# Entering a feed-forward layer with two plain hidden tiles instead of four: normalisation read from the banks, sums added by transfers

## The chip, the cores and the metric

The kernel runs on one core of one Trainium2 chip. The metric is the time of one execution on the device in microseconds (us). Nothing else runs on the core, and the inputs lie in HBM.

## What is computed

Two layers over 512 tokens with 1024 features each, all in float32. Each layer is a half-step feed-forward network (FFN), a mixer of three kinds of heads, and a second half-step FFN:

```python
def swiglu(h, w_in, w_out):
    gate, up = jnp.split(h @ w_in, 2, axis=-1)
    return (jax.nn.silu(gate) * up) @ w_out

for l in range(DEPTH):                      # DEPTH = 2
    x = x + 0.5 * swiglu(rms_norm(x, ffn1_norm[l]), ffn1_w_in[l], ffn1_w_out[l])
    h = rms_norm(x, mix_norm[l]) @ w_mix_in[l]
    y = concat([short_conv(h), hgrn2(h), fox_attention(h)])
    x = x + y @ w_mix_out[l]
    x = x + 0.5 * swiglu(rms_norm(x, ffn2_norm[l]), ffn2_w_in[l], ffn2_w_out[l])
```

`w_in` is 1024x5632 (2816 gate columns and 2816 up columns), `w_out` is 2816x1024. `rms_norm` divides each token by the root of its mean square over the 1024 features and multiplies by a gain for each feature.

## The kernel before, in words

The residual stream lies in SBUF with features on partitions: `xT` is eight tiles j of 128 features x 512 tokens. Float32 accuracy is kept with three products of the reduced type float32r: every operand is parted into a high part (a cast on ACT) and a low part (a subtraction on DVE), and `mm3` (L316 to L339) issues high x high (L328), high x low (L336) and low x high (L337). Two helpers make these pairs: `parted` (L314 ACT, L315 DVE) for streamed weights, `prepare` in `halved` (L810 ACT, L812 DVE) for weights that are sums.

An FFN has 22 hidden tiles of 128. Two ways to compute them stand in the code:

- **Plain.** A pair of hidden tiles takes 8 feature tiles x 4 banks (two gate, two up) x 3 = 96 matmuls of 512 tokens (`stream_steps`). The operand is x times gain (`scaled`, L402 to L415: ACT L408, DVE L409), and the division by the root of the mean square comes afterwards, from the bank (`clear`, `values`). So a plain pair needs no norm before it starts.
- **Halved.** A pair is computed by a scheme of seven block products P1 to P7 over halves of the features and of the tokens, in the order P1, P2, P6, P5, P7, P3, P4 (`ORDER_IN`); each product is 8 x 3 = 24 matmuls of 256 tokens, 168 for the pair. It needs the normed x cut into four quarters X[a,b] (a: half of the features, b: half of the tokens), sums of these quarters, and sums of four quarters of the weights. `plan` orders the products and gives loads, accumulating DMAs and sums their due places; `LEAD = 3` says that weights are parted three products ahead.

The first tiles of each FFN are plain because the norm of x isn't ready yet: they are the "covered" tiles. The very first FFN covers six (`FIRST`, its own function `cover`); the other three (FFN 2 of layer 0, FFN 1 and FFN 2 of layer 1) cover four, by `enter` (L583 to L699). These three places are called entries here.

An entry, before:

1. The last four banks of the phase ahead (the mixer's output projection, or the FFN's) hold the new contribution to features 512 to 1023. DVE adds each to `xT` (L1230 or L502), then ACT squares it (L424), DVE adds the square into `sqacc` (L425), and `scaled` makes the gained pair.
2. TensorE runs the first plain pair from the gained x. After the sixth of its eight feature tiles the sum of squares is parted (L438) and two matmuls with a matrix of 1/1024 give the mean to every partition (L447). ACT takes Ln, Exp and a square (L277) and DVE finishes the reciprocal root `inv` (L431 to L433).
3. During the second plain pair DVE multiplies the four quarters (L619, 16 instructions), adds them (L642), and ACT and DVE part P1, P2, P5, P6 (`high` L632, `low` L635 and L637). The raw weights of the first halved pair (four tiles of 512 KB) are loaded by SP (L863) and one is added to another by an accumulating DMA from POOL (L786).
4. The halved products begin. P7, P3 and P4 are made beside them (`self.entry`, by product number), and so are the values of the covered tiles.

What fixes the order: TensorE's, ACT's and DVE's instructions are queued in program order, with hand-set order among those marked by `follow`; an instruction waits for semaphores at the head of its queue. All PSUM banks are allotted in two groups of four (`next4`). Of the halved products P1, P6, P7 and P4 go into one bank (called a), P2 into a second (c), P5 and P3 into a third (b); ACT reads bank a after P1 (L919), and DVE reads it after P7 (L934), each before the next product may write it. Parted weights lie in a ring of three tiles `hl`, streamed weights in a ring of two tiles `st`.

Of the kernel before, what the change touches and what calls it, by code (L numbers as in the profile page):

```python
# [9 lines left out]
F32 = mybir.dt.float32  # L10
# [30 lines left out]
FIRST = 6  # L41
# [21 lines left out]
def plan(covered):  # L63
# [27 lines left out]
    for u in dict.fromkeys((k, w) for k, w, _ in seq):  # L91
# [68 lines left out]
class Trunk:  # L160
# [255 lines left out]

    def squared(self, j, xj, pool):
# [25 lines left out]

    def end_norm(self, bank, pool, parts, keep=False):
        nc = self.nc
        for n, part in enumerate(parts):
            nc.tensor.matmul(bank, self.ones_mean, part, start=n == 0, stop=n == 1)  # L447
# [10 lines left out]
    def ffn(self, w_in, w_out, next_gain, covered, begin=None, out=None):  # L458
        nc = self.nc
        tc = self.tc  # L460
        with tc.tile_pool(name=self.n("ffn"), bufs=1) as fp:
# [26 lines left out]
            for dg in range(2):  # L488
                banks = self.next4()

                def parts(k, kk, dg=dg):
# [4 lines left out]
                    [(bk, slice(c, c + P), None) for bk, c in zip(banks, (0, 128, 256, 384))],  # L496
                    parts, self.last_hidden, nf,
                )
                for i in range(4):
# [6 lines left out]
                    if next_gain is not None:  # L506
                        self.norm_part(j, fp)
# [75 lines left out]
    def enter(self, fp, w_in, then):  # L583
        nc = self.nc
        H = T // 2
        A, V = (lambda i, e=e: self.follow(e, i) for e in "av")

        def stream(f, banks, given):
            def parts(k, kk):
                r = slice(k * P, (k + kk) * P)  # L590
                return [w_in[r, f * P : (f + 2) * P], w_in[r, FF + f * P : FF + (f + 2) * P]]

            return self.stream_steps(
                [(bk, slice(c, c + P), None) for bk, c in zip(banks, (0, 256, 128, 384))],
                parts, self.xact, KD, given=given,
            )

        ba = self.next4()
        first = stream(0, ba, lambda k: k == KD - 2)
        for _ in range(4):  # L600
            next(first)
        parts = self.parted_norm(fp, ("g1", "g1"), 2, True)
        nb = self.bank("pt" if self.ntog % 2 == 0 else "po")
        bb = self.next4()
        second = stream(2, bb, lambda k: True)
        self.ngain = self.const.tile([P, KD], F32, tag="ngain", name=self.n("ngain"))
        A(nc.scalar.activation(self.ngain, self.gain, AF.Copy, scale=-1.0))
        next(second)
        self.end_norm(nb, fp, parts, True)
        self.table(SILU)  # L610
        next(first, None)
        next(then)
        X, self.xc, lows = {}, {}, {}

        def quarter(a, b):
# [28 lines left out]
        def both(name):  # L644
            high(name)
            lows[name]()

        def row():
            next(second)
            next(second, None)  # L650

        cleared = {}

        def clear(f, i):
            banks = bb if f else ba
            cleared[f, i] = self.clear(fp, banks[2 * i], banks[2 * i + 1], True)

        def values(f, i):
            self.values(fp, f, i, *cleared.pop((f, i)), True)

        quarter(0, 0)
        high("P1")
        quarter(1, 0)
        lows["P1"]()
        next(second)
        next(second)
        high("P2")
        quarter(0, 1)
        lows["P2"]()
        quarter(1, 1)  # L670
        next(second)
        next(second)
        add((0, 0), (0, 1))
        high("P5")
        clear(0, 0)
        lows["P5"]()
        next(second)
        next(second)
# [1244 lines left out]
```

## Time and profile before

| what | value |
|---|---|
| median of 3 runs | 1805.61 us (1802.3 to 1805.83) |
| the profiled execution | 1801.38 us |
| its span, first to last instruction | 1799.6 us |
| TensorE busy | 1792.0 us (100%) |
| DVE, ACT, POOL busy | 1430.1 us (79%), 1001.0 us (56%), 176.6 us (10%) |
| HBM, mean over the span | 126 GB/s |

The profile names TensorE PE, VectorE DVE, ScalarE ACT, GpSimd POOL and SyncE SP. PEld is PE's loading of held operands, which overlaps PE. A row of a group shows the line of the kernel, the engine, the operation, the tiles written and read, shape, count, then busy time and the mean in ns of one, then idle time before it and who ended it. A row of a timeline shows start in us from the start of the span, duration, and the same names; "x4" means four instructions merged into a row. Matmuls overlap in a pipeline, so the rate is read from one start to the next, not from the duration. L numbers in the profile are those of the kernel before.

The three entries lie at about 570 to 650 us, 895 to 975 us and 1460 to 1540 us of the span.

### The profile page before, as it was taken

The page shows a single profiled execution, that of the slowest core. Times are in us where ns is not written, and L with a number is a line of the kernel's source. Part 1 is how long each engine was busy: PE and PEld are TensorE (multiplying, and loading weights), DVE is VectorE, ACT ScalarE, POOL GpSimd, SP SyncE. Part 2 cuts the span into 40 slices and gives each one's busy share as a digit, 9 for nine tenths or more (in the row PEclk, how much of TensorE's full clock was granted, in tenths as well). Part 3 has the DMA queues.
Part 4 walks back from the last instruction along what each step waited for, and adds up shares of the span by engine and source line. Part 5 has one row for each costly group of instructions (what it writes and reads, how often), then busy time and mean ns, then how long its engine had stood idle before and what let it go on. Part 6 is the DMA issues. An engine that isn't in the chain of part 4 may idle for free.

```text
span 1799.6 us, 34747 instructions
## 1 busy us (share of the span) xinstructions
PE 1792.0 (100%) x14271; PEld 1681.0 (93%) x14271; DVE 1430.1 (79%) x2006; ACT 1001.0 (56%) x1445; POOL 176.6 (10%) x184
## 2 busy tenths in 40 slices
PE   9999999999999999999999999999999999999999
PEld 7899999899888899999889999998998888999997
DVE  9889787676888798879679887876868879888793
ACT  5455554464776465556446555555547755555551
POOL 0011120100000002112001111201000000020210
PEclk9999999999999999999999999999999999999999
DMA  7659793233433857868265786913334346597762
GB/s 207 180 133 196 169 188 97 71 82 84 106 98 108 222 130 170 194 163 166 82 207 133 169 185 175 187 65 83 78 85 116 89 144 179 141 185 190 160 133 94
DMA packets 244638, 254.09 MB, mean 141 GB/s; under 512 B 18904, under 2 KB 228576, under 8 KB 244480
## 3 DMA queue, kind: packets, MB, share of 16 engines
q1 hardware_dynamic: 189424, 182.38, 33.7%
q0 software_dynamic: 54752, 69.23, 23.8%
q8 instruction: 112, 1.84, 0.4%
q14 instruction: 46, 0.38, 0.1%
q10 hardware_dynamic: 304, 0.27, 0.0%
HBM read 223.98 MB, written 2.10 MB: 126 GB/s over the span
## 4 chain that ended last, share of the span: by engine, by line
PE 94%; DVE 2%; ACT 2%; DMA 1%; issue 1%; SPq 0%; POOL 0%; ACTq 0%; DVEq 0%; POOLq 0%
PE mm L328 14%; PE mm L336 14%; PE mm L337 14%; PE sc L328 6%; PE sc L336 6%; PE sc L337 6%; PE pt L336 6%; PE pt L328 6%; PE pt L337 6%; PE po L328 4%; PE po L336 4%; PE po L337 4%; PE po L1654 1%; PE pt L1698 1%; PE pt L1352 1%
## 5 line engine op out<-in xcount | busy, mean ns | idle before, releaser
L810 ACT CAST hl<-w 128x1024 fp32r<-128x1024 f32 x322 | 336.8, 1050 | 305.9 <-PE mm L337 80.4
L812 DVE TENSOR_TENSOR hl<-w,hl 128x1024 fp32r<-128x1024 f32 x322 | 391.8, 1220 | 96.7 <-ACT hl L810 96.7
L315 DVE TENSOR_TENSOR hl<-st,hl 128x512 fp32r<-128x512 f32 (+3 forms) x196 | 162.5, 830 | 116.2 <-ACT hl L314 115.0
L314 ACT CAST hl<-st 128x512 fp32r<-128x512 f32 (+3 forms) x196 | 143.1, 732 | 174.3 <-PE po L337 66.8
L328 PE MATMUL mm<-xc,hl 128*128 128x256 f32 (+1 forms) x733 | 201.3, 276 | 0.0
L336 PE MATMUL mm<-xc,hl 128*128 128x256 f32 x728 | 201.2, 276 | 0.0
L337 PE MATMUL mm<-xc,hl 128*128 128x256 f32 x728 | 201.0, 276 | 0.0
L328 PE MATMUL sc<-xc,hl 128*128 128x256 f32 (+1 forms) x532 | 146.0, 276 | 0.0
L336 PE MATMUL sc<-xc,hl 128*128 128x256 f32 x528 | 146.0, 276 | 0.0
L337 PE MATMUL sc<-xc,hl 128*128 128x256 f32 x528 | 145.8, 276 | 0.0
L328 PEld LDWEIGHTS mm<-xc,hl 128*128 128x128 f32 x733 | 137.4, 188 | 0.2
L337 PEld LDWEIGHTS mm<-xc,hl 128*128 128x128 f32 x728 | 136.7, 188 | 0.0
L336 PEld LDWEIGHTS mm<-xc,hl 128*128 128x128 f32 x728 | 136.7, 188 | 0.0
L328 PE MATMUL pt<-xc,hl 128*128 128x256 f32 (+1 forms) x482 | 132.6, 276 | 0.0
L336 PE MATMUL pt<-xc,hl 128*128 128x256 f32 x480 | 132.6, 276 | 0.0
L337 PE MATMUL pt<-xc,hl 128*128 128x256 f32 x480 | 132.5, 276 | 0.0
L328 PE MATMUL mm<-x,hl 128*128 128x512 f32 x272 | 107.6, 396 | 0.0
L336 PE MATMUL mm<-x,hl 128*128 128x512 f32 x272 | 106.3, 391 | 0.0
L337 PE MATMUL mm<-x,hl 128*128 128x512 f32 x272 | 106.2, 390 | 0.0
L328 PEld LDWEIGHTS sc<-xc,hl 128*128 128x128 f32 x532 | 99.7, 188 | 0.2
L336 PEld LDWEIGHTS sc<-xc,hl 128*128 128x128 f32 x528 | 99.1, 188 | 0.0
L337 PEld LDWEIGHTS sc<-xc,hl 128*128 128x128 f32 x528 | 99.1, 188 | 0.0
(517 smaller groups left out, 5575.0 us busy)
## 6 DMA issues: line engine op xcount, KB each, us to landing
w<-in_ffn_w_in_dram SPq DMA_DIRECT2D x140, 512.0 KB, 5.1
w<-in_ffn_w_out_dram SPq DMA_DIRECT2D x64, 512.0 KB, 5.2
w<-in_ffn_w_out_dram POOLq DMA_DIRECT2D x56, 512.0 KB, 7.2
st<-in_w_mix_in_dram SPq DMA_DIRECT2D x88, 256.0 KB, 2.8
st<-in_ffn_w_in_dram SPq DMA_DIRECT2D x70, 256.0 KB, 3.1
w<-in_ffn_w_in_dram POOLq DMA_DIRECT2D x35, 512.0 KB, 8.9
w<-S POOLq DMA_DIRECT2D x35, 512.0 KB, 4.7
st<-in_ffn_w_out_dram SPq DMA_DIRECT2D x24, 512.0 KB, 5.3
```

Of the source, the lines that this page charges most:

```text
L314: a = nc.scalar.copy(hi, src[:, c : c + w])
L315: b = nc.vector.tensor_sub(lo, src[:, c : c + w], hi)
L328: i = nc.tensor.matmul(acc[:, c], ah, bh[:, c], start=first and c.start == 0, stop=False, skip_group_check=True,)
L336: nc.tensor.matmul(acc, a, b, start=False, stop=False, skip_group_check=True)
L337: i = nc.tensor.matmul(acc, c, d, start=False, stop=last, skip_group_check=True)
L810: A(nc.scalar.copy(hi, src))
L812: return lambda: V(nc.vector.tensor_sub(lo, src, hi))
L1352: nc.tensor.matmul(bank[hh][rows[par], at + x * n : at + (x + 1) * n], held[rows[hh], c * CH : (c + 1) * CH], moving(rows[hh], c), start=T ...
L1654: nc.tensor.matmul(self.ob[:, t0 + u * P : t0 + 2 * P], V[:, j, h % 4].rearrange("p a d -> p (a d)"), part[:, j, u:, :].rearrange("p i t - ...
L1698: nc.tensor.transpose(tb[:, j * P : (j + 1) * P], p[:, j * P : (j + 1) * P], self.ident)
```

## The change

The three entries cover one plain pair instead of two (`COVERED = 2`), so that one more pair of each of these FFNs is halved. To that end:

- **Old x in the last banks** (`seed`): before the last four banks of the phase ahead accumulate, ACT copies the old `xT` of that feature tile into the bank (three banks of four after the mixer, four after the FFN, there with a factor of 2), and the matmuls add to it. The sum then stands in the bank.
- **Squares from the banks** (`norm_late`): ACT squares the bank itself, DVE adds the squares, and the copy of the bank to `xT` (`arrive`) comes later on ACT. For the last bank after the mixer DVE still adds to `xT` first. The gained pairs of features 512 to 1023 (`scaled`) move from ahead of the mean to behind the reciprocal root.
- **The mean** is put after the second feature tile of the one plain pair.
- **Quarters**: for two of four, ACT multiplies by the gain (`grown`, four instructions of 128x256) and DVE by `inv` in one instruction of 128x1024 (`multiplied`); the other two are made as before (`made`).
- **Early weights**: the loads of the first halved pair's raw weights are issued right after the first part of the plain pair. The FFN's pool of tiles gets `reuse_waits="tile"`.
- **Sums by accumulating transfers**: the sum S3 of the weights, and the sum X[0,1] + X[1,1] (`carry`), are made by accumulating DMAs on POOL's queue instead of DVE.

The core of the diff:

```diff
-FIRST = 6
+FIRST, COVERED = 6, 2
@@ plan
                 when(-1, 6, "adds", u)
-                when(0, 2, "total", u, "S3")
+                if covered == FIRST:
+                    when(0, 2, "total", u, "S3")
@@ new
+    def seed(self, js, banks, scale):
+        for j, bk in zip(js, banks):
+            if scale == 1.0:
+                self.nc.scalar.copy(bk, self.xT[:, j, :])
+            else:
+                self.nc.scalar.activation(bk, self.xT[:, j, :], AF.Copy, scale=scale)
+
+    def norm_late(self, js, pool, banks, scale, update=None):
...
+        for j, bk in zip(js, banks):
+            own = update is not None and j == js[-1]
+            if own:
+                self.follow("v", update(j, bk))
...
+            src = self.xT[:, j, :] if own else bk
+            self.follow("a", nc.scalar.activation(sq, src, AF.Square, scale=scale))
+            self.follow("v", nc.vector.tensor_add(self.sqacc, self.sqacc, sq))
+            self.arrive[j] = lambda j=j, bk=bk, own=own: own or self.follow(
+                "a", nc.scalar.activation(self.xT[:, j, :], bk, AF.Copy, scale=scale)
+            )
@@ ffn
-        with tc.tile_pool(name=self.n("ffn"), bufs=1) as fp:
+        with tc.tile_pool(name=self.n("ffn"), bufs=1, reuse_waits="tile") as fp:
@@ enter
+        def grown(a, b):
+            X[a, b] = t = fp.tile([P, 4, H], F32, tag=f"r{2 + 2 * a + b}", name=self.n("xn"))
+            for k in range(4):
+                i = 4 * a + k
+                A(nc.scalar.activation(
+                    t[:, k, :], self.xT[:, i, b * H : (b + 1) * H], AF.Copy,
+                    scale=(self.gain if a == b else self.ngain)[:, i : i + 1],
+                ))
+
+        def multiplied(a, b):
+            V(nc.vector.tensor_mul(
+                X[a, b], X[a, b], self.inv[:, b * H : (b + 1) * H].unsqueeze(1).to_broadcast([P, 4, H])
+            ))
...
+        def carry(x, y):
+            self.follow("g", nc.gpsimd.dma_start(X[x], X[y], accum_op=ALU.add))
...
+        next(plain)
+        next(then)
+        self.arrive[7]()
+        self.arrive[6]()
+        norm = self.parted_norm(fp, ("g1", "g1"), 2, True)
+        self.mean(nb, norm)
+        next(plain)
+        next(plain)
+        self.arrive[4]()
+        self.arrive[5]()
+        self.factor(nb, fp, True)
+        grown(0, 0)
+        multiplied(0, 0)
+        for j in (4, 5):
+            self.scaled(j, self.xT[:, j, :], True)
+        next(plain)
+        next(plain)
+        for j in (6, 7):
+            self.scaled(j, self.xT[:, j, :], True)
+        next(plain)
         high("P1")
-        quarter(1, 0)
+        grown(1, 0)
+        low = prepared(0)
         lows["P1"]()
...
+        multiplied(1, 0)
+        low()
+        self.given["total"]()
+        self.given["add"](0, 2)
         high("P2")
...
+        made(0, 1)
         lows["P2"]()
...
         add((0, 0), (0, 1))
+        low()
         high("P5")
...
+        made(1, 1)
         lows["P5"]()
...
+        carry((0, 1), (1, 1))
         add((0, 0), (1, 1))
         high("P6")
-        self.given["total"]()
         lows["P6"]()
...
         next(then)
...
         self.entry = {
-            0: lambda: both("P7"),
-            1: lambda: (both("P3"), add((0, 0), (1, 0))),
-            3: lambda: high("P4"),
-            7: lambda: values(0, 1),
-            9: lambda: clear(2, 0),
-            10: lambda: values(2, 0),
-            13: lambda: values(2, 1),
+            0: lambda: (high("P7"), lows["P7"]()),
+            1: lambda: (high("P3"), lows["P3"]()),
+            2: lambda: (add((0, 0), (1, 0)), high("P4"), lows["P4"]()),
+            8: lambda: clear(0),
+            9: lambda: values(0),
+            11: lambda: clear(1),
+            12: lambda: values(1),
         }
-        self.between = {4: lambda: lows["P4"](), 13: lambda: clear(2, 1)}
+        self.between = {}
```

How it moves instructions is shown at two places of the first entry. First PE's queue around the mean, `ones_mean` being the matrix of 1/1024, `x2` the gained pairs of the feature tiles, `hl` the parted weights. Before:

```order
L328 MATMUL pt_974_6817<-x2_965_6791,hl_980_6881 128x512
L336 MATMUL pt_974_6817<-x2_965_6791,hl_980_6881 128x512
L337 MATMUL pt_974_6817<-x2_965_6791,hl_980_6881 128x512
L447 MATMUL po_985_6918<-sh_983_6914,ones_mean_72 128x512
L447 MATMUL po_985_6918<-sh_984_6915,ones_mean_72 128x512
L328 MATMUL sc_971_6814<-x2_967_6798,hl_982_6911 128x512
```

and of the kernel with the change:

```order
L329 MATMUL pt_970_6805<-x2_948_6708,hl_974_6812 128x512
L337 MATMUL pt_970_6805<-x2_948_6708,hl_974_6812 128x512
L338 MATMUL pt_970_6805<-x2_948_6708,hl_974_6812 128x512
L469 MATMUL po_971_6806<-sh_979_6849,ones_mean_72 128x512
L469 MATMUL po_971_6806<-sh_980_6850,ones_mean_72 128x512
L329 MATMUL sc_967_6802<-x2_950_6715,hl_982_6858 128x512
```

The mean stood behind 72 matmuls of the plain pair (six feature tiles) and now stands behind 24 (two).

Second DVE's queue ahead of the third halved product, P6. `xc` are parted sums of quarters (P1, P2, P5, P6 in this order), `xn` the quarters, `S` the sum of weights that P6 takes, `gi`, `ui`, `hq` the values of a covered tile, `w` raw weights. Before, from the last streamed weights to the low part of P6's weights:

```order
L315 TENSOR_TENSOR hl_1017_7101<-st_1016_7098,hl_1017_7101 128x1024
L642 TENSOR_TENSOR xn_1000_6976<-xn_1000_6976,xn_1009_7029 128x1024
L798 TENSOR_TENSOR S_1020_7132<-w_996_6967,w_997_6969 128x1024
L637 TENSOR_TENSOR xc_1019_7130<-xn_1000_6976,xc_1018_7129 128x1024
L812 TENSOR_TENSOR hl_1021_7135<-w_997_6969,hl_1021_7135 128x1024
L812 TENSOR_TENSOR hl_1022_7138<-w_999_6973,hl_1022_7138 128x1024
L572 TENSOR_TENSOR gi_1023_7141<-pt_973_6816,inv_995_6937 128x512
L573 TENSOR_TENSOR ui_1024_7142<-pt_974_6817,inv_995_6937 128x512
L642 TENSOR_TENSOR xn_1008_7023<-xn_1008_7023,xn_1009_7029 128x1024
L713 TENSOR_TENSOR hq_1026_7150<-gi_1014_7068,ui_1015_7069 128x256
L710 SCALAR_TENSOR_TENSOR hq_1027_7152<-gi_1014_7068,ui_1015_7069 128x256
L812 TENSOR_TENSOR hl_1028_7154<-S_1020_7132,hl_1028_7154 128x1024
```

and of the kernel with the change, from the product with `inv` that makes the second quarter to the low part of P6's weights:

```order
L648 TENSOR_TENSOR xn_997_6977<-xn_997_6977,inv_987_6897 128x1024
L862 TENSOR_TENSOR hl_998_6982<-w_976_6841,hl_998_6982 128x1024
L848 TENSOR_TENSOR S_999_6987<-w_975_6839,w_976_6841 128x1024
L656 SCALAR_TENSOR_TENSOR xn_1003_6996<-xT_76,ngain_972_6807,inv_987_6897 128x256 x4
L674 TENSOR_TENSOR xc_1001_6991<-xn_997_6977,xc_1000_6990 128x1024
L679 TENSOR_TENSOR xn_988_6902<-xn_988_6902,xn_1003_6996 128x1024
L862 TENSOR_TENSOR hl_1002_6994<-w_978_6845,hl_1002_6994 128x1024
L656 SCALAR_TENSOR_TENSOR xn_1006_7007<-xT_76,gain_630_5444,inv_987_6897 128x256 x4
L674 TENSOR_TENSOR xc_1005_7005<-xn_988_6902,xc_1004_7004 128x1024
L679 TENSOR_TENSOR xn_988_6902<-xn_988_6902,xn_1006_7007 128x1024
L674 TENSOR_TENSOR xc_1008_7016<-xn_988_6902,xc_1007_7015 128x1024
L862 TENSOR_TENSOR hl_1010_7022<-S_999_6987,hl_1010_7022 128x1024
```

The weights of the second plain pair (`st`) and the values of covered tiles (`gi`, `ui`, `hq`) are gone from this stretch. The low parts of the three halved weights and their sum S stand between the quarters now. Between the reciprocal root and the first of these rows stand seven more: a 128x1024 product with `inv` (the first quarter), four gained pairs of 128x512, one streamed weight of 128x1024 and P1's low part of 128x1024.

More of the change, by code (lines that the diff above doesn't have):

```diff
@@ L642, in add @@
             V(nc.vector.tensor_add(X[x], X[x], X[y]))
[L644 to L661, printed above, removed]
+        held = {}
@@ L1229, in add @@
             def add(j, bank):
[L1230 removed]
+                return nc.vector.tensor_add(self.xT[:, j, :], bank, self.xT[:, j, :])
             def most():
```

106 lines of the change are left out of this document (52 added, 54 removed).

## The prediction

> **What bounds the kernel now.** I read the page first, for the bound over the whole span, then PE's waits.
>
> ```profile
> PE 1792.0 (100%) x14271; PEld 1681.0 (93%) x14271; DVE 1430.1 (79%) x2006; ACT 1001.0 (56%) x1445; POOL 176.6 (10%) x184
> PEclk9999999999999999999999999999999999999999
> PE pt L1698 <- DVE QA L1600: 1.3, 2, 0.6
> PE mm L1815 <- DVE z L1802: 1.2, 1, 1.2
> ...
> PE po L447 <- ACT sh L438: 0.2, 1, 0.2
> ```
>
> PE is busy in the whole span, and no wait of PE is longer than 1.2 us (the last column). So TensorE is the bound, any matmul that goes is worth its time in the queue, and any new wait of PE is paid in full. Therefore I next read PE's timeline through the first entry, to get its fixed points.
>
> ```profile
> 578.11 0.39 PE L328 MATMUL sc<-x,hl 128*128 128x512 f32 x1
> ...
> 594.44 0.62 PE L447 MATMUL po<-sh,ones_mean 128*128 128x512 f32 x2
> ...
> 622.12 0.33 PE L328 MATMUL sc<-xc,hl 128*128 128x128 f32 x2
> ...
> 638.58 0.28 PE L328 MATMUL sc<-xc,hl 128*128 128x256 f32 x1
> ...
> 641.29 0.28 PE L328 MATMUL pt<-xc,hl 128*128 128x256 f32 x1
> ```
>
> 578.11 is the start of the plain cover, called c below; 594.44 the mean; 622.12 the first halved product P1; 638.58 the seventh, P4; 641.29 the next pair's P1. Cover: 622.12 - 578.11 = 44.01 us for 2 x 96 + 2 matmuls, 0.227 us each. A halved pair: 641.29 - 622.12 = 19.17 us; one product (638.58 - 622.12) / 6 = 2.74 us. A plain pair is 96 x 0.227 = 21.8 us.
>
> How near are the engines that feed PE there? I asked for the busy times from the reciprocal root to P1, and for DVE's timeline over that stretch.
>
> ```profile
> 599.10:622.10 23.00, 23.00 (x103) 19.05 (x102) 22.75 (x33) 10.00 (x11) 1.06 (x2) 1.00 0.74 215
> 598.34 0.69 DVE L433 TENSOR_TENSOR inv<-nr,nt 128x512 f32<-128x512 f32 x1
> 599.06 1.67 DVE L619 SCALAR_TENSOR_TENSOR xn<-xT,gain,inv 128x256 f32<-128x256 f32 x4
> ...
> 618.38 2.35 DVE L812 TENSOR_TENSOR hl<-w,hl 128x1024 fp32r<-128x1024 f32 x2
> ...
> 623.65 1.22 DVE L812 TENSOR_TENSOR hl<-S,hl 128x1024 fp32r<-128x1024 f32 x1
> ...
> 636.59 0.68 DVE L934 TENSOR_TENSOR u<-u,sc 128x512 f32<-128x512 f32 x1
> ```
>
> The third busy figure is DVE's: 22.75 of 23.00 us. An average of 79% hides this: between `inv` (done at 598.34 + 0.69 = 599.03) and the halved products DVE has no room at all. What P6, the third product, needs last from DVE is the low part of S, ready at 623.65 + 1.22 = 624.87; P6's turn on PE is 622.12 + 2 x 2.74 = 627.60. **The margin today is 2.7 us**, behind 25.8 us of DVE work.
>
> **The change part by part.**
>
> *Matmuls.* In each entry 96 matmuls of 512 become 168 of 256: 21.8 - 19.1 = 2.7 us less on PE (a pair that follows the first takes 7 x 2.72, rounded 19.1). Three entries: **-8.1 us**. Seeding takes none away: an accumulation starts on the old value instead of clearing.
>
> *The tail of the phase ahead.* DVE's adds to `xT` of three or four banks go, and ACT's copies come. Neither engine is the bound there; the mean only has to be ready. I check this in the first entry, the tightest, where each of the last four banks ends with only three matmuls. Its rows:
>
> ```profile
> 575.59 1.06 ACT L314 CAST hl<-st 128x1024 fp32r<-128x1024 f32 x1 [0.58 <-PE po L337]
> 576.68 1.23 DVE L315 TENSOR_TENSOR hl<-st,hl 128x1024 fp32r<-128x1024 f32 x1
> 577.82 1.88 DVE L1230 TENSOR_TENSOR xT<-mm,xT 128x512 f32<-128x512 f32 x3
> ...
> L424 ACT ACTIVATE sq<-xT 128x512 f32<-128x512 f32 x4 | 2.5, 621 | 0.5 <-DVE xT L1230 0.5
> L438 ACT CAST sh<-sqa 128x512 fp32r<-128x512 f32 x1 | 0.6, 622 | 0.5 <-issue 0.5
> ```
>
> A DVE instruction of 512 follows another after (1.88 - 0.68) / 2 = 0.60 us. DVE is free at 577.9; three adds of squares (the third waits for ACT) end at 579.8, the last bank's own add at 580.4, its square on ACT at 581.1, its sum at 581.8, the high part at 582.4, the low part at 583.1. PE reaches the mean after 24 matmuls, at 578.11 + 5.45 = 583.56. It fits by 0.4 us, so the mean costs PE nothing; cover gone, each further us there would be a us. Ahead of it, in the attention's last steps, the seeds stand between ACT's casts that PE reads; three of 0.62 us, of which I charge 0.2 us for each of the two entries after a mixer (bounds 0, as ACT's idle gaps hold them, and 1.9, all three): +0.4 us.
>
> *The reciprocal root* comes earlier: before, 599.03 - 594.44 = 4.6 us after the mean's start; now at c + 5.45 + 4.6 = **c + 10.0** (before c + 20.9). In the first entry ACT's copies to `xT` may add 0.2.
>
> *The work behind it.* By the order of DVE's queue, from `inv` to the low part of S in P6's weights there are now thirteen instructions of 128x1024: two products with `inv`, one streamed weight, four low parts of xc, three of hl, S, two adds. One follows another after 2.35 - 1.22 = 1.13 us: 14.7 us. Four gained pairs of 512, moved here from ahead of the mean, and the eight quarter instructions that stay:
>
> ```profile
> L409 DVE SCALAR_TENSOR_TENSOR x<-xT,gain,x 128x512 fp32r<-128x512 f32 x4 | 3.0, 744 | 0.0
> L632 ACT CAST xc<-xn 128x1024 fp32r<-128x1024 f32 x4 | 4.2, 1049 | 9.0 <-DVE xn L642 9.0
> ```
>
> A gained pair follows after 0.744 less the overlap of 0.08, 0.66 us: 2.6 us. A quarter instruction after (1.67 - 0.48) / 3 = 0.40: 3.2 us. One real hole is in the chain: P6's sum of quarters ends on DVE, then ACT casts its high part (1.05 us), and only then can DVE subtract: 1.1 us. With the last instruction's tail and small waits for ACT, 0.3. Sum: 14.7 + 2.6 + 3.2 + 1.1 + 0.3 = **21.9 us**, so P6's weights are ready at c + 31.9. The broadcast product with `inv` isn't in the trace; as a 128x1024 of two operands from SBUF I take 1.13 us, bounds 0.8 (two quarter rows) and 1.6 (the four that it replaces), +-0.8 us on the sum.
>
> PE's turn for P6: c + 98 x 0.227 + 2 x 2.74 = **c + 27.7**. P1 and P2 themselves are fed in time (by the same sum P1's low parts are done by c + 18.7 against c + 22.2, P2's by c + 24.8 against c + 25.0). So PE waits **4.2 us** ahead of P6. The same in other words: cover shrinks by 21.8, `inv` comes 10.9 earlier, DVE's work shrinks by 25.8 - 21.9 = 3.9; the margin of 2.7 becomes 2.7 - 10.9 + 3.9 = -4.3.
>
> P6 has a second lock of the same date: it writes bank a, which ACT must first read (L919 before), and this copy stands behind the casts of P6's and P5's weights in ACT's queue.
>
> ```profile
> 622.38 1.05 ACT L810 CAST hl<-S 128x1024 fp32r<-128x1024 f32 x1 [0.38 <-PE po L337]
> 626.17 0.59 ACT L919 ACTIVATE g<-sc 128x512 f32<-128x512 f32 x1
> ```
>
> ACT casts xc right after the sum of quarters (c + 29.7), then two weights at 0.95 us steps and the copy of 0.59: c + 31.9 too.
>
> *After P6.* P4 writes bank a again, after DVE has added P7's result from it to `u2`. In DVE's queue eight instructions of 1024 (P5's weights; P7's, P3's and P4's operands and weights; one sum of quarters) and two of 512 stand between P6's weights and the end of that add: 8 x 1.13 + 0.60 + 0.68 = 10.3, and holes of 1.1 (P4's sum, then ACT's cast) and about 0.8 (P3's cast behind a silu): 12.2. The bank is free at c + 31.9 + 12.2 = c + 44.1; PE's turn without any wait is c + 22.2 + 16.5 = c + 38.7. So by P4 PE is late by **5.4 us in all**, of which 4.2 came at P6. From there the queue recovers: later pairs need less of DVE than PE's 19 us.
>
> *Transfers.* Before, loads and accumulation had 20 us to spare; their rows:
>
> ```profile
> 587.10 2.44 SPq L863 DMA_DIRECT2D w<-in_ffn_w_in_dram  x4
> 592.43 1.37 POOL L786 DMA_DIRECT2D w<-in_ffn_w_in_dram  x1 [57.23 <-DMA w<-in_ffn_w_in_dram]
> ...
> w<-in_ffn_w_in_dram POOLq DMA_DIRECT2D x35, 512.0 KB, 8.9
> w<-S POOLq DMA_DIRECT2D x35, 512.0 KB, 4.7
> ```
>
> Now SP may issue the loads at c + 0.8, when the streamed weights ahead of them in its queue have gone (their ring is freed at 577.9). The first is landed 592.43 - 587.10 = 5.3 us after issue, c + 6.1, the accumulation 8.9 us later, c + 15; DVE takes S at about c + 18.6. Hidden, by 3.6 us. S3 by transfer starts after that, lands by c + 30, needed for P7 at c + 33 or later: hidden. `carry` is issued on POOL's queue when X[1,1] is made (c + 26.4) and takes 4.7 to 8.9 us: c + 31.1 to c + 35.3; ACT's cast of P7 waits for it, and P7, P3, P4's casts queue behind. At 4.7 it is hidden by the late P6; at 8.9 everything up to P4 shifts by some 3 us. I take 0.4 us an entry, nearer to the SBUF-sourced row (w<-S), which is the same kind.
>
> *The sum.* Per entry -2.7 + 5.4 + 0.4 = +3.1 us; three entries +9.3, tails +0.4: **+9.7 us**. Against the profiled execution (1801.38: its span of 1799.6 and 1.8 around it) that is 1811.1; the median of the runs is 4.2 above that execution, so I predict 1805.6 + 9.7 = **1815.3 us**.
>
> *The clock.* PEclk is 9 in all forty slices, and no PE wait exceeds 1.2 us; the 4.2 us ahead of P6 would be the first long one. The Trainium skill, "TensorE: Matmul & The Clock Gate", section "Why this matters for your kernels", wants no idle gap over about 3 us between bursts of matmuls, else the clock falls to half. No run here shows it. By that rule the sum would be the one of the clock rival below.
>
> **The rivals.**
>
> - *DVE keeps up* (faster). If P6's operands are ready by c + 27.7, only the matmuls count: -8.1 + 0.4, so 1797.9 us. It needs 4.2 us less than the rows give, by cheaper broadcast products (0.8 at most by my bounds) and by a mean earlier than its place, which PE's order forbids. For it: the moved work is off the ends of the cover, and my sum hangs on one entry's rows. Chance 0.16.
> - *P6 alone waits.* If ACT's holes after P6 close, PE catches P4 without more waiting: 3 x (4.2 - 2.7) + 0.4 = +4.9, 1810.5 us. Chance 0.13.
> - *A wash.* If the wait is about as long as the gain, 2.7 us, within 3.6 us of before: 1805.6. It needs the sum of DVE's work 1.5 to 2.7 us shorter than 21.9; the bounds above allow 0.8. Chance 0.08.
> - *The clock falls after the wait.* P6's 24 matmuls take twice 2.72 us; 1.2 us of it lies under the wait for P4, so 1.5 an entry: +4.5, 1819.8 us. Against it, one matmul runs when the high parts come. This is the rule of the Trainium skill's page named above. Chance 0.08.
> - *Transfers come late.* `carry` at 8.9 us, or raw weights that wait for the mixer's buffers: about 2 us an entry more, 1821 us. Chance 0.05.
>
> **How the numbers follow.** The forecast, a wait at P6 and a rest at P4, has 0.50. A measurement of this kernel tells about 0.2%, 3.6 us, from no change. Faster: 0.16, the first rival. Same: 0.08. Slower: 0.50 + 0.13 + 0.08 + 0.05 = 0.76. The range leaves out the faster rival and a little above: the forecast's own range is +-5 us (0.8 us an entry for the broadcast products, 0.7 for ACT's holes), 1810 to 1820; downwards it takes in the P6 rival and the wash, upwards the clock and late transfers: 1801 to 1822.
>
> **What would show it.** In the profile after: PE idle of about 4 us ahead of the third halved product in each entry, ended by DVE's low part of S or ACT's copy of bank a, and 1 to 1.5 us ahead of the seventh, ended by DVE's add to `u2`; the mean at c + 5.5 with no wait; `inv` at c + 10; DVE without a gap from there on; 216 more matmuls. I am wrong if PE runs through P6 without a wait, if the mean itself waits, or if ACT or a transfer is what DVE waits for.

## The result, and the profile after

| | before | with the change |
|---|---|---|
| median | 1804.88 us (1802.3 to 1805.83, 4 runs) | 1835.98 us (1834.3 to 1836.7, 4 runs) |
| profiled execution, its span | 1801.38, 1799.6 us | 1835.45, 1833.7 us |

The ratio is 1.0173, 95% interval [1.0156, 1.0191]: the change makes the kernel 31.1 us slower. The forecast was 9.7 us slower, with 1822 us as its upper end. Ratios and intervals use fast executions alone; one of the four of e3_split below ran at a clock of 0.56 (3007 us), and the median given there, 1834.45 us, would be 1833.28 without it. From here on L numbers are those of the kernel with the change (L329, L337, L338 are the three matmuls of `mm3`, L469 the mean, L860 and L862 the cast and the subtraction of halved weights, L969, L978 and L981 ACT's copies of banks).

First the page's line of busy times, and PE's waits (us in total, times, longest us):

```profile
PE 1802.4 (98%) x14487; PEld 1698.3 (93%) x14487; DVE 1435.3 (78%) x1978; ACT 1033.4 (56%) x1507; POOL 190.1 (10%) x196
```

```profile
PE mm L329 <- ACT g L969: 13.6, 3, 5.1
PE mm L329 <- ACT u L981: 5.1, 3, 2.5
PE po L329 <- DVE hq L760: 2.7, 3, 0.9
PE po L329 <- ACT g L978: 1.3, 3, 0.5
PE pt L1751 <- DVE QA L1653: 1.2, 2, 0.6
```

216 matmuls more, as said. The longest single wait before was 1.2 us, in a mixer; the last row is of a mixer too and stood in the list before, with 1.3 us in total. The four rows above it are new, each with three cases, one for each entry. Next PE's timeline through the first entry; the brackets give idle time and who ended it:

```profile
580.06 0.39 PE L329 MATMUL sc<-x,hl 128*128 128x512 f32 x1
...
585.51 0.62 PE L469 MATMUL po<-sh,ones_mean 128*128 128x512 f32 x2
...
602.67 0.33 PE L329 MATMUL mm<-xc,hl 128*128 128x128 f32 x2
...
612.70 0.39 PE L329 MATMUL mm<-xc,hl 128*128 128x256 f32 x1 [4.29 <-ACT g L969]
...
613.96 0.42 PE L329 MATMUL mm<-xc,hl 128*128 128x256 f32 x1
614.18 0.41 PE L337 MATMUL mm<-xc,hl 128*128 128x256 f32 x1
...
625.27 0.39 PE L329 MATMUL mm<-xc,hl 128*128 128x256 f32 x1 [2.51 <-ACT u L981]
...
642.41 0.38 PE L329 MATMUL po<-xc,hl 128*128 128x256 f32 x1 [0.54 <-ACT g L978]
...
654.49 0.36 PE L329 MATMUL po<-xc,hl 128*128 128x256 f32 x1 [0.91 <-DVE hq L760]
```

c is 580.06, the mean is at c + 5.45 without a wait, P1 at c + 22.6. From start to start, less the 0.113 us of one matmul, PE loses 4.45 us ahead of P6 (612.70), 2.67 ahead of P3 (625.27), 0.70 and 1.07 in the two pairs behind. After P6's wait matmuls start 0.22 us apart (613.96, 614.18) instead of 0.113. That is the clock. The table by stretch has the granted clock as its seventh figure (1.00 is full):

```profile
612.70:613.70 1.00, 1.00 (x8) 1.00 (x9) 1.00 (x1) 0.00 (x0) 0.00 (x0) 1.00 1.12 213
613.70:617.10 3.40, 3.40 (x18) 3.40 (x17) 1.74 (x3) 1.99 (x2) 0.00 (x0) 0.50 1.10 185
617.10:620.00 2.90, 2.90 (x28) 2.90 (x27) 2.39 (x3) 2.70 (x4) 0.00 (x0) 1.00 0.39 62
948.20:951.60 3.40, 3.09 (x14) 3.09 (x15) 3.40 (x5) 2.37 (x4) 0.00 (x0) 0.50 1.08 155
1521.60:1528.50 6.90, 4.57 (x21) 4.57 (x22) 5.59 (x6) 4.58 (x6) 0.03 (x1) 0.51 1.09 193
```

It is 0.50 for 3.4 us in the first entry, from one microsecond after the wait ends. In the second entry it is 0.50 for 3.4 us as well, but from 0.3 us before the wait ends (P6 starts at 948.51), and in the third 0.51 for 6.9 us, from 2.3 us before (P6 starts at 1523.93). And there is a loss with no wait at all. PE's timeline at 660 us, a product of 24 matmuls from the first row to the second, in full clock:

```profile
660.10 0.28 PE L338 MATMUL mm<-xc,hl 128*128 128x256 f32 x1
...
662.92 0.28 PE L338 MATMUL mm<-xc,hl 128*128 128x256 f32 x1
```

2.82 us, 117.5 ns a matmul, where before it is 2.72 us. This goes on from 654.7 to 697.0 us.

So the first 110 us from P1, worked out from all starts, lose 12.9 us (before: 0.3): waits 8.9 (4.45 + 2.67 + 0.70 + 1.07), half clock 1.9, and 2.1 in steps under 0.08 us, the 118 ns among them. The other entries lose 12.4 and 12.5. Less 0.3 and less the 2.7 us gained in matmuls that is 9.9, 9.3 and 9.5 us an entry, 28.7 of the 34.1 us that lie between the two profiled executions. Of the rest 2.0 lie ahead of the first FFN's mean at 33.1 us, before any edit: executions differ there by about that much (30.8 to 32.8 us in the runs below). The other 3.4 are spread over the covers, the mixers and the stretches behind the entries, 1.3 of them at 118 ns behind the second.

### The profile page after: what moved, and what is told of

Read it like the earlier page. It is cut to its first block, busy times and chain, and to the rows that moved or that the text cites. A ratio compares the mean times of both kernels' runs of the same rounds, so it can differ in the third digit from the quotient of the medians.

```text
span 1833.7 us, 35228 instructions
## 1 busy us (share of the span) xinstructions
PE 1802.4 (98%) x14487; PEld 1698.3 (93%) x14487; DVE 1435.3 (78%) x1978; ACT 1033.4 (56%) x1507; POOL 190.1 (10%) x196
## 5 line engine op out<-in xcount | busy, mean ns | idle before, releaser
L860 ACT CAST hl<-w 128x1024 fp32r<-128x1024 f32 x340 | 355.8, 1048 | 329.2 <-PE mm L338 122.6
L862 DVE TENSOR_TENSOR hl<-w,hl 128x1024 fp32r<-128x1024 f32 x340 | 414.8, 1222 | 117.2 <-ACT hl L860 116.8
L329 PE MATMUL mm<-xc,hl 128*128 128x256 f32 (+1 forms) x1595 | 442.6, 279 | 18.7 <-ACT g L969 13.6
L337 PE MATMUL mm<-xc,hl 128*128 128x256 f32 x1584 | 441.8, 279 | 0.0
L338 PE MATMUL mm<-xc,hl 128*128 128x256 f32 x1584 | 441.1, 278 | 0.0
L329 PEld LDWEIGHTS mm<-xc,hl 128*128 128x128 f32 x1595 | 301.5, 189 | 20.2 <-ACT g L969 14.2
L338 PEld LDWEIGHTS mm<-xc,hl 128*128 128x128 f32 x1584 | 300.6, 190 | 0.0
L337 PEld LDWEIGHTS mm<-xc,hl 128*128 128x128 f32 x1584 | 300.1, 189 | 0.0
L316 DVE TENSOR_TENSOR hl<-st,hl 128x512 fp32r<-128x512 f32 (+2 forms) x184 | 148.2, 806 | 110.4 <-ACT hl L315 109.1
L315 ACT CAST hl<-st 128x512 fp32r<-128x512 f32 (+2 forms) x184 | 130.8, 712 | 158.9 <-PE po L338 48.2
L329 PE MATMUL po<-xc,hl 128*128 128x256 f32 x545 | 151.3, 278 | 4.0 <-DVE hq L760 2.7
L337 PE MATMUL po<-xc,hl 128*128 128x256 f32 x544 | 150.8, 277 | 0.0
L338 PE MATMUL po<-xc,hl 128*128 128x256 f32 x544 | 150.7, 277 | 0.0
L329 PE MATMUL pt<-m,hl 128*128 128x256 f32 x448 | 124.0, 277 | 0.0
L337 PE MATMUL pt<-m,hl 128*128 128x256 f32 x448 | 124.0, 277 | 0.0
L338 PE MATMUL pt<-m,hl 128*128 128x256 f32 x448 | 124.0, 277 | 0.0
L338 PE MATMUL sc<-m,hl 128*128 128x256 f32 x448 | 123.8, 276 | 0.0
L329 PE MATMUL sc<-m,hl 128*128 128x256 f32 x448 | 123.8, 276 | 0.0
L337 PE MATMUL sc<-m,hl 128*128 128x256 f32 x448 | 123.8, 276 | 0.0
L329 PEld LDWEIGHTS po<-xc,hl 128*128 128x128 f32 x545 | 102.3, 188 | 5.1 <-issue 3.2
L338 PEld LDWEIGHTS po<-xc,hl 128*128 128x128 f32 x544 | 102.4, 188 | 0.0
L337 PEld LDWEIGHTS po<-xc,hl 128*128 128x128 f32 x544 | 102.2, 188 | 0.0
```

The lines of the kernel that those rows point to most:

```text
L315: a = nc.scalar.copy(hi, src[:, c : c + w])
L316: b = nc.vector.tensor_sub(lo, src[:, c : c + w], hi)
L329: i = nc.tensor.matmul(acc[:, c], ah, bh[:, c], start=first and c.start == 0, stop=False, skip_group_check=True,)
L337: nc.tensor.matmul(acc, a, b, start=False, stop=False, skip_group_check=True)
L338: i = nc.tensor.matmul(acc, c, d, start=False, stop=last, skip_group_check=True)
L860: A(nc.scalar.copy(hi, src))
```

## The experiments

The first theory, called the chain: what PE waits for are dates that DVE and ACT set by their queues since the reciprocal root, since the cover is 21.8 us shorter and the work isn't. Its rivals: the secondary losses (clock, pitch) are the main cost; transfers are; or the new head of the entry (seeds, squares from banks, early weights) is. "Above before" is the ratio less one, times 1802.6 us. In the rows of a run the L numbers are those of its own kernel, shifted by its edit.

### Keeping the clock (e1_warm)

```diff
+            if u == ("I", covered) and p == "P2" and self.entry:
+                work[u, "b"] = idle = bank(kind)
+                for _ in range(24):
+                    self.follow("p", nc.tensor.matmul(
+                        idle[:, :H], held[0][:, 0, :P], held[1][:, 0, :], start=True, stop=True,
```

> The kernel with the change, and 24 idle matmuls of 256 tokens (2.7 us) between the second and the third halved product of each entry; their results are thrown away, everything else is computed as before. Chain theory (PE's waits are dates set by DVE and ACT, and lateness before a date is lost only once): the granted clock stays full, so the third product no longer loses 1.6 us, but the wait ahead of the sixth product, whose date PE doesn't set, grows by as much; the total falls by 0 to 3 us, to 1833 to 1836 us. Clock theory (the fallen clock is a loss of its own): 1.6 us in the first two entries and 3.2 in the third come back, 6.4 us, 1829.6 us. If the clock falls all the same, the gap isn't what lowers it.

1834.75 us, ratio 1.0177 [1.0161, 1.0194]. Its waits, and the clock in the first entry and in the second:

```profile
PE mm L329 <- ACT g L977: 7.1, 3, 3.9
PE mm L329 <- ACT u L989: 6.2, 3, 2.8
```

```profile
611.30:615.00 3.70, 3.65 (x32) 3.65 (x33) 1.81 (x3) 1.76 (x3) 0.00 (x0) 1.00 1.08 199
...
949.30:953.00 3.70, 3.69 (x22) 3.69 (x23) 3.70 (x4) 2.68 (x4) 0.00 (x0) 0.69 0.76 121
```

The clock stays full in the first and third entry, where 1.7 us of gap are left, and nothing is won: the wait ahead of P3 goes from 2.67 and 1.62 to 2.93 us in both, and more is lost ahead of P7. In the second entry another wait (below, the negated gain) left 3.9 us and the clock fell. The clock theory falls: while P3 is locked, the fallen clock costs nothing of its own.

### P4's cast behind the copy of bank b (e2_p4later)

```diff
-            2: lambda: (add((0, 0), (1, 0)), high("P4"), lows["P4"]()),
+            2: lambda: add((0, 0), (1, 0)),
+            3: lambda: (high("P4"), lows["P4"]()),
```

> The kernel with the change, and the operand of the seventh product (P4) is cast one step later, behind ACT's copy of bank b. Chain theory: the copy that the sixth product (P3) waits for no longer stands behind a cast that waits for DVE's sum; the waits of 2.7, 1.3 and 1.6 us ahead of it go, and P4's operand is ready at about its turn: 5.6 us less, 1830.4 us, the wait ahead of the third product unchanged at 4.5 to 5.2. Passing-on theory (DVE's arrears are what counts, and the next product waits instead): 1835 to 1837 us.

1827.38 us, 1.0129 [1.0114, 1.0144]: 23.3 us above before instead of 31.1. All of its waits on bank copies of the entry:

```profile
PE mm L329 <- ACT g L970: 14.0, 3, 5.4
PE po L329 <- DVE hq L761: 2.4, 3, 0.9
PE po L329 <- ACT g L979: 1.3, 3, 0.5
```

The row of bank b is gone, P6's is unchanged. The gain is larger than the waits (5.6 us): with them go most of the stretches at 118 ns (small steps 7.0 to 2.3 us in the three entries). So the second lock is an order of two instructions in ACT's queue. These are the rows of ACT's timeline in the kernel with the change:

```profile
612.06 0.59 ACT L969 ACTIVATE g<-mm 128x512 f32<-128x512 f32 x1
614.36 1.06 ACT L669 ACTIVATE xc<-xn 128x1024 fp32r<-128x1024 f32 x1 [1.71 <-issue]
...
622.74 1.06 ACT L669 ACTIVATE xc<-xn 128x1024 fp32r<-128x1024 f32 x1 [2.43 <-DVE xn L679]
623.70 1.03 ACT L860 CAST hl<-w 128x1024 fp32r<-128x1024 f32 x1
624.63 0.59 ACT L981 ACTIVATE u<-mm 128x512 f32<-128x512 f32 x1
```

P5's result had stood in bank b since about 620 us. Its copy (L981) queued behind P4's cast at 622.74, and that waited for DVE's sum.

### The first matmul of each pair in two pieces (e3_split)

```diff
-                kind == "I" and p == "P1" and w in (covered, *PARTED),
+                kind == "I" and p == "P1",
```

> The kernel with the change, and the first matmul of every halved input pair goes in two pieces of 128 tokens (so far those of the covered pair and of two more in each FFN). Pitch theory (a wait leaves PE in a phase in which a matmul of 256 takes 118 ns instead of 113, until pieces of 128 end it): the stretches at 118 ns, 6.8 us in all, shrink to those up to the next pair, by about 5 us, 1831 us. If the pitch has another cause (the clock, the supply of data): no change, 1836 us, and the stretches stay.

1834.45 us, 1.0167 [1.0150, 1.0184]. The same kind of product, at the same place:

```profile
658.28 0.28 PE L338 MATMUL mm<-xc,hl 128*128 128x256 f32 x1
...
661.00 0.28 PE L338 MATMUL mm<-xc,hl 128*128 128x256 f32 x1
```

2.72 us for 24 matmuls. Of the 6.8 us that the stretches at 118 ns cost in the kernel with the change 1.6 are left, so pieces of 128 do end them. But all losses of the three entries fall by only 2.5 us (37.8 to 35.3): half clock and other small waits took the rest. The ratio can't tell it from nothing.

### P7's sum on DVE (e4_dve_add)

```diff
-        carry((0, 1), (1, 1))
         add((0, 0), (1, 1))
         high("P6")
+        add((0, 1), (1, 1))
```

> The kernel with the change, and the sum X[0,1] + X[1,1] is made by DVE while ACT casts the operand of the third product, where DVE had a hole of 1.15 us, instead of by a transfer. Chain theory with a late transfer: the third product waits as before (0.1 us more); ACT's cast of the fifth product's operand no longer waits 1.7 us for the transfer, and the wait ahead of the sixth product falls from 2.7 to about 1.2 us in the first entry and as much in the others: 3 to 4.5 us less, 1832 us. If the transfer is hidden: 1836 us, the waits unchanged.

1833.12 us, 1.0168 [1.0151, 1.0185]. P3's wait in its list of waits, and the transfer's row in the kernel with the change (KB, median us from issue to landing):

```profile
PE mm L329 <- ACT u L981: 3.3, 3, 1.1
```

```profile
xn<-xn POOLq DMA_DIRECT2D x1, 512.0 KB, 7.0
```

The transfer takes 7.0 us, so that it lands at 614.3 and P7's cast waits 1.71 us for it (ACT's row at 614.36 above; its releaser is shown as "issue"). On DVE the sum costs nothing there, and P3's wait becomes 1.27 us in each entry (from 2.67, 1.26 and 1.62). That is 1.7 us of PE in all: the late transfer is real and small, and the 3 to 4.5 us that I expected aren't there. The profiled execution had 10.4 us ahead of P6 in the second entry instead of 5.24, from the negated gain (e6_ngain below).

### One more instruction on DVE (e5_extra)

```diff
         lows["P5"]()
+        lows["P5"]()
```

> The kernel with the change, and DVE makes the low part of P5's operand twice in each entry, one instruction of 1.13 us more ahead of P6's operand; nothing else depends on it. Chain theory (DVE's work since the reciprocal root dates the third product and all behind it): the wait ahead of the third product grows by 1.1 us in each entry, 4.45 to 5.6, the wait ahead of the sixth keeps its size, and the total grows by about 3.4 us against the kernel with the change, to 1839 us. If ACT or a transfer sets these dates: no change, 1836 us, the wait stays at 4.45.

1833.3 us, 1.0169 [1.0154, 1.0184]. Its waits:

```profile
PE mm L329 <- ACT g L970: 16.4, 3, 5.6
PE mm L329 <- ACT u L982: 3.9, 3, 1.9
```

P6's wait grew by 1.26 us in the first entry and 1.28 in the third (5.71 and 5.73 us; the two equal instructions start 1.27 apart), and only 0.2 in the second, where the negated gain (next point) had held P6's cast 1.2 us beyond DVE's sum anyway. So DVE's work dates P6, one for one. But the total did not grow: P3's wait shrank by 0.6, 0.2 and 0.4. P7's cast stood 11.7 us after P1 in the kernel with the change and 12.1 here, with P6's date 1.25 later: behind P6 the transfer (7.4 us here) holds the date, and DVE idled 1.66 us for it before. This part of my expectation failed.

### The negated gain in its place (e6_ngain)

```diff
-        nc.scalar.activation(self.ngain, self.gain, AF.Copy, scale=-1.0)
+        A(nc.scalar.activation(self.ngain, self.gain, AF.Copy, scale=-1.0))
```

> The kernel with the change, and the copy of the negated gain (ACT, 128x8) is kept in its place at the start of each entry; in the change it is free, and the third entry's copy stands in ACT's queue inside the second entry, ahead of the cast of P6's operand, where it waits for the load of a later gain (done at 944.9 us, 1.2 us after DVE's sum). Theory: the wait ahead of the third product in the second entry becomes that of the others, 4.45 instead of 5.24 us, the first and third entries stay; 0.8 us less in the profile (more in executions in which the load comes later), 1835 us. Rival: the second entry's longer wait has another cause, and it stays at 5.2.

1830.36 us, 1.0160 [1.0145, 1.0175]. ACT's timeline in the second entry, with the change and then here:

```profile
944.93 0.21 ACT L696 ACTIVATE ngain<-gain 128x8 f32<-128x8 f32 x1 [5.22 <-DMA gain<-in_ffn_norm_dram]
945.04 1.03 ACT L669 CAST xc<-xn 128x1024 fp32r<-128x1024 f32 x1
```

```profile
942.34 1.05 ACT L669 CAST xc<-xn 128x1024 fp32r<-128x1024 f32 x1 [4.06 <-DVE xn L679]
```

With the change, a copy of 8 columns for the third entry was left free by the edit and came to stand ahead of P6's cast in the second; it waits for a load of 4 KB. In place, the cast waits for DVE alone, and P6's wait in that entry is 3.93 us instead of 5.24. The theory held, with 1.3 us where 0.8 was expected; in the third entry P3's wait grew from 1.62 to 2.46 us, which the theory doesn't explain, and the ratio can't tell the total from that of the kernel with the change. In e4_dve_add's profile the same copy waited until 946.54, 6.4 us after DVE's sum, which is that run's 10.4 us. The full diff drops the `A(...)` that keeps ACT's order; I read past it, and the extract of the diff shown with the change leaves that line out.

### All mends together (e7_mended), and P5 ahead of P6 (e8_swap)

e7_mended has the edits of the runs above but e5_extra's, and `clear(1)`, `values(1)` at steps 15 and 16 instead of 11 and 12. e8_swap has these edits without idle matmuls, and:

```diff
+ORDER_COVERED = ("P1", "P2", "P5", "P6", "P7", "P3", "P4")
...
+        for p in (ORDER_COVERED if f == covered == COVERED else ORDER_IN)
...
         add((0, 0), (1, 1))
+        next(then)
         high("P6")
         lows["P6"]()
+        add((0, 1), (1, 1))
```

> The kernel with the change and all mends together: P4's operand cast one step later, the negated gain in its place, the first matmul of each halved input pair in two pieces, the sum for P7 on DVE in the hole, the second hidden tile's values of the plain pair four steps later, and the 24 idle matmuls that keep the clock. Chain theory: the wait of 4.45 us ahead of the third product stays in each entry, P4 waits up to 1.5 us for DVE, and little else is left: 1817 to 1822 us, still slower than before. If the secondary losses (clock, pitch, passed-on waits) were the main cost: 1810 us or less.

> As the mended kernel, but without idle matmuls, and the third and fourth product of the covered pair change places: P5, whose operand DVE has 3.5 us earlier, runs ahead of P6; the low part of P6's weights fills DVE's hole. Chain theory (DVE's whole work up to P4 is the bound, not P6's place): the wait of 4.45 us breaks into several of 0.5 to 2 us, no gap exceeds 3 us and the clock stays full, but their sum in an entry stays at 3.5 to 5 us, and the time is that of the mended kernel within 3 us, 1815 to 1822. Place theory (only P6's operand comes too late): 1.5 us are left of 4.45, 9 us less than the mended kernel, about 1810.

e7_mended: 1819.14 us, 1.0092 [1.0077, 1.0107], 16.6 us above before. e8_swap: 1822.04 us, 1.0110 [1.0094, 1.0127]. The first row is from e7_mended's waits, the two others from e8_swap's (where L numbers are two higher and L957 is ACT's copy of bank a after P6):

```profile
PE mm L329 <- ACT g L978: 4.2, 3, 1.6
```

```profile
PE mm L331 <- ACT g L957: 9.9, 3, 3.3
PE mm L339 <- DVE xc L676: 1.9, 3, 0.6
```

Mended, P6's 4.45 us stay (2.7 us of idle matmuls and 1.75 of gap), P3 doesn't wait and P4 under 0.4 us. So about half of the loss, 14.5 of 31.1 us, lay outside P6's wait; the 1810 us or less that would have made it the main cost isn't reached. Swapped, P5 and P6 lose 1.4 us, but then P7 follows P6 in bank a and waits 3.48 us for the copy, which stands behind P3's cast on ACT. The sum, 4.9 us in the first entry, is as expected; that no gap passes 3 us isn't, and the clock fell in two entries. Since this lock is of another kind than DVE's work, the run doesn't settle what P6's place alone is worth.

### Less of DVE ahead of P6 (e9_less)

```diff
-        made(0, 1)
+        multiplied(0, 1)
...
-        made(1, 1)
+        multiplied(1, 1)
         lows["P5"]()
+        low = prepared(2)
         add((0, 0), (1, 1))
         high("P6")
+        low()
         lows["P6"]()
         add((0, 1), (1, 1))
```

(`grown` for both on ACT ahead of these, and ACT's copy of bank a after P1 ahead of P5's weights.)

> The mended kernel without idle matmuls, and with less of DVE ahead of P6: the gain goes onto all four quarters on ACT, so that DVE multiplies each in one instruction of 1.13 us instead of four of 0.40 (0.9 us less), the low part of P6's weights fills DVE's hole (1.1 less), and ACT copies bank a ahead of P5's weights. Chain theory: the wait ahead of the third product falls from 4.45 to about 2.3 us and no gap reaches 3 us, so the clock stays full without idle matmuls; of these 2.2 us only the 0.9 of work that is gone stay gained, since the hole's filling moves work past P6, and P3 and P4 wait for it: 2.7 us less than the mended kernel, 1816 us. If the wait at P6 were the only lock: 6.5 us less, 1813 us. If DVE isn't the lock: the wait stays 4.45 us.

1816.24 us, 1.0077 [1.0062, 1.0092]: 2.7 us less than e7_mended by the ratios, the size that the chain says. P6 loses 2.29, 1.83 and 2.32 us, and in two entries P7 and P4 wait 0.6 to 0.8 us each. The agreement is partly luck: P7 waits where I had expected P3, and in the first entry the clock fell all the same, for 1.9 us. Its waits:

```profile
PE mm L329 <- ACT g L960: 4.0, 3, 1.5
...
PE mm L329 <- ACT g L989: 1.6, 3, 0.5
...
PE mm L337 <- DVE xc L674: 1.1, 3, 0.4
PE mm L329 <- DVE u L995: 1.1, 2, 0.7
```

The last row is the lock that I had named for P4 (the add to `u2`): it comes up once P6's is short.

### The whole change with the old cover (e10_cover4, e11_cover4)

```diff
-FIRST, COVERED = 6, 2
+FIRST, COVERED = 6, 4
...
+        plain = stream(0, ba, lambda k: k >= 4)
+        second = stream(2, bb, lambda k: True)
```

(with the second pair's steps between the quarters, and `clear` and `values` where the kernel before has them)

> The change with the old cover: seeds, squares from the banks, the early mean, gained quarters, early weights and sums by transfers are kept, but each entry runs two plain pairs as before (COVERED = 4), with the values of the covered tiles at their old places and the negated gain in its place. The matmuls are those of before. Chain theory: with 21.8 us more of cover no product waits, the new head costs nothing but 0 to 1 us an entry, and the time is that of before within 3 us, 1802 to 1808 us against 1804.9. If the head itself (seeds, transfers, the loads beside the cover) costs: 1812 us or more.

e10_cover4 took 1816.91 us, 1.0079 [1.0064, 1.0093], and says nothing on the theories: the transfer stood in the wrong place, so that P1 took the sum in place of the raw quarter and waited for it. This kernel doesn't compute the layer.

> As the kernel e10_cover4, with the transfer that makes S3 put behind the cast of the first product's weights instead of ahead of it. (There the first product of each entry took the sum in place of the raw quarter, so that its output wasn't the reference's, and waited 2.2 to 2.6 us for the transfer.) Chain theory: no product of an entry waits, and the time is that of before within 3 us, 1802 to 1808 us. If the head itself costs (seeds, transfers, loads beside the cover): 1810 us or more.

e11_cover4: 1804.45 us, ratio 1.0007 [0.9998, 1.0016]. Its waits of PE, the longest first:

```profile
PE pt L1766 <- DVE QA L1668: 1.2, 2, 0.6
PE mm L1883 <- DVE z L1870: 1.2, 1, 1.2
PE sc L1699 <- DMA QA<-QB: 1.1, 2, 0.7
```

No wait is in an entry; these three are the mixer's, as before. The new head with all its seeds, early loads and transfers costs -0.4 to 2.9 us. What costs is the plain pair that is missing beside it.

## Why the prediction was wrong, and what of it was right

- **Matmuls, mean, reciprocal root.** Right: 216 more matmuls; the mean at c + 5.45 without a wait; `inv` at 590.51, c + 10.45, against c + 10.0.
- **P6.** Right in place, cause and size: 4.45, 5.24 and 4.45 us against 4.2. DVE's timeline ends the chain at 612.65, c + 32.6, against c + 31.9, and the broadcast product took 1.23 us, as I took it:

```profile
590.61 1.23 DVE L648 TENSOR_TENSOR xn<-xn,inv 128x1024 f32<-128x1024 f32 x1
...
610.29 1.23 DVE L674 TENSOR_TENSOR xc<-xn,xc 128x1024 fp32r<-128x1024 f32 x1 [1.15 <-ACT xc L669]
611.43 1.22 DVE L862 TENSOR_TENSOR hl<-S,hl 128x1024 fp32r<-128x1024 f32 x1
```

  The releaser that PE's rows name, ACT's copy of bank a, is the second lock of the forecast; it ends at 612.65 too (L969 in ACT's rows above, 612.06 + 0.59), and both hang on DVE's sum of quarters. e5_extra and e9_less move this wait by what they add to and take from DVE, both ways.
- **"By P4 PE is late by 5.4 us in all."** This step failed. In the first entry PE is 9.0 us late at P4 (it starts at 628.12, against P1 + 16.46). I had followed bank a through P7 to P4, and not bank b: P3 writes it, ACT must first copy P5's result, and in ACT's queue that copy stood behind a cast that waits for DVE. The entry's table of steps puts P4's cast at step 2, where the table of before has it at 3: two lines of the diff. e2_p4later undoes it, for 7.9 us. The wait that I did forecast there, 1.2 us ahead of P4 for DVE's add to `u2`, is 0.17 us in e2_p4later's first entry and not seen in the others.
- **"From there the queue recovers."** Failed: 0.70 and 1.07 us in the pairs behind the first, and 1.6 us in the stretch at 118 ns that follows. I had given them nothing. The two waits stand two products behind the values of the plain pair's tiles (steps 9 and 12), and with the second of these four steps later in e7_mended its wait came four products later. Why the same kind of values cost nothing in the kernel before, no run shows.
- **The clock rival** came true in each entry, with 1.9 us in the first where I had 1.5, at a chance of 0.08. I had it as another way for the time to come out; it came on top of the rest. The Trainium skill, "TensorE: Matmul & The Clock Gate", section "Why this matters for your kernels", wants no idle gap over about 3 us; after gaps of 4.3 to 5.1 us the trace agrees, while e9_less shows the clock fall after less (last section). I should have held that rule for likely, since my own forecast had a wait of 4.2 us. Yet it isn't the cause: e1_warm keeps the clock and wins nothing.
- **`carry`.** I took 4.7 us, it took 7.0 beside the other transfers, within my bounds of 4.7 to 8.9. By e4_dve_add it is worth 1.7 us in all; 1.2 was charged.
- **What I said would make me wrong**, a transfer that ACT or DVE waits for, was there twice (`carry`, and the gain's load in the second entry), and each was worth 1 to 3 us.
- **The sum.** -2.7 + 5.4 + 0.4 = 3.1 us an entry became -2.7 + 12.6 = 9.9 in the first. The sign and the first term held; I stopped following PE after the second lock. The 6.8 us between 5.4 + 0.4 and 12.6 are 0.25 more at P6, 2.67 at P3 in place of the 1.2 at P4 and the 0.4 for `carry`, and three terms that the sum put at nothing: 1.9 of half clock, 1.8 in the pairs behind, and 1.75 in small steps, most of it at 118 ns. e1_warm shows that these don't simply add: with the half clock gone the waits for P3 and P7 were longer by as much. Before's margin of 2.7 us, read as one lock's, was the margin of a whole queue: e9_less, with every mend but the idle matmuls, is still 13.9 us above before.

Not settled: whether a short cover can win at all with still less work on DVE in the entry. No version of these runs did, and none beats the kernel before.

## What to carry to other kernels

A shorter head start is paid by each engine that used it: count the work between the start signal and each date, and follow every buffer that the bound engine writes next, not just the first late one. The waits don't end with the late product: follow the bound engine until its rows show no more of them (here two pairs of products behind). When a table of steps is rewritten, check for each instruction what now stands ahead of it on its own queue, small unordered ones too.

## What the hardware showed that I had not expected

- After some waits, matmuls of 256 start 117.8 ns apart instead of 113.3 at full clock, for up to 42 us in the kernel with the change, without any wait; a matmul in two pieces of 128 ends it (e3_split), and so does another wait. From 654.7 to 697.0 us that is 359 matmuls and 1.6 us. Why, no run shows.
- The clock fell after each gap of 3.5 us and more. It also fell once in e9_less, after 1.64 and 0.65 us with one matmul between (0.66 in the mean from 608 to 612 us), and did not after 3.39 us in the third entry of e8_swap (1.00 from 1521 to 1525 us). The times fit a beat of 3.41 us: each stretch of half clock in an entry lasts one, two or three beats (3.4, 6.8 or 10.2 us), and in the kernel with the change the falls at 613.71, 948.21 and 1521.65 us are 98 and 168 beats apart. In the kernel with the change and in e1_warm to e9_less the full clock fell at the end of every beat in which PE had waited 2.1 us or more in all, and of none with 1.9 us or less. In e9_less the two gaps lie in one beat, 2.29 us together; in e8_swap the end of a beat parts the gap into 1.9 and 1.5 us.
- An accumulating transfer of 512 KB within SBUF took 7.0 us beside the loads, where before's transfers of that kind took 4.7 at the median.
